# Decoder trunk on one core: B turned by transposes, norm weights applied from PSUM, x loaded over 128 partitions, two low parts and the first load of h moved

## The chip, the cores and the metric

The kernel runs on one core of a Trainium2 chip. The metric is the device time of one execution in microseconds (us). Five engines work side by side, each through its own instructions in order: TensorE (PE, matmuls and transposes, with weight loads as PEld), VectorE (DVE), ScalarE (ACT), GpSimd (POOL) and SyncE (SP, which here only issues DMAs). They meet through semaphores. PE writes to PSUM, of which this kernel uses eight banks of 128x512 float32; POOL works on SBUF alone.

## The reference, cut to what matters

A decoder of two layers over 256 tokens with 2048 features, all in float32: an S5 state-space mixer with GLU, a SwiGLU, sliding-window attention, a second SwiGLU, a norm ahead of each and one at the end. The change lies in the first layer's mixer and at the start of its GLU:

```python
hn = rmsnorm(h, norm_mix[0])                       # x * rsqrt(mean(x*x) + eps) * g
dt = exp(log_step); lb = exp(lam * dt)             # 128 groups x 64 states, complex
q  = (lb - 1) / lam                                # = (n_re, n_im) * conj(lam) / |lam|^2
bu = einsum('blgc,gpc->blgp', hn, q * b)           # 16 channels a group into 64 states
s  = associative_scan(lb, bu)                      # s[l] = lb * s[l-1] + bu[l]
y  = Re(einsum('blgp,gcp->blgc', s, c)) + d_skip * hn
gl = gelu(y) @ w_glu                               # 2048 x 4096
h  = x + gl[:, :2048] * sigmoid(gl[:, 2048:])
```

## The kernel before, in words

**The mixer** is `s5` (from L182). The tokens are cut into 64 chunks of L = 4. For each group the four tokens of a chunk are folded into one input of the state: X holds B times the powers of lb, so the state is scanned once a chunk, 63 steps, in two halves `hf` of the states. The order of work is written out by hand: inside `s5` the engines are wrapped in `Ordered`, whose instructions keep program order while `on` is true (so most rows of this stretch carry its line, L210); where it is off a scheduler places them.

The steps, with the names of the diff and the profile:
- `Bn` is B as loaded (128 groups on partitions), real, imaginary and real again. `turned_b` (L388) turns it into `B1` and `B2` (states on partitions), four channels to a PSUM bank `ps`. Before, each of its 32 products is a matmul of Bn with `wd[:, c]`, the identity scaled by one column of the norm weight `wg`; 16 ACT copies (L291) make `wd`. So the norm weight sits in B. ACT evicts each bank, with a sign (`sgn`) for B2.
- `LP` are the powers of lb, computed on DVE (L320 to L358) from `exp(ls)`. `q_` is q, from the inverse square `iv` (L366 to L378). PE turns LP into `LR`, `LI` and `pl`; ACT copies `LRs` and `LPT`.
- `real_parts(t)` on POOL: three products `tmp` of LRs with B1 for quarter t. `imag` on DVE: products `pa` of LI (in PSUM) with B2. `token(t, j)` adds the two into X; `last_token(t)` is a copy of B1 on ACT.
- `xk` is x by chunk and token, its two halves of features on partitions 0 to 63 and 64 to 127. `squares(j)` on ACT sum the squares of token j, `both` adds the two halves of a row on PE (`rb`), and a chain on DVE and ACT gives the scale `r0`. `scaled(hf, j)` writes r0 times xk to `xs`; `tokens(t, b)` turns xs on PE (`pu`) and ACT copies it to `U`.
- `turned_x` (PE `px`, ACT `xt`), `added` (PE `pv`) and `kept` (copy to V) follow for four quarters t and four blocks b. `kept(1, 3)` completes the first half's inputs V0, `kept(3, 3)` the second's, V1.
- `step(hf)` (L552 to L557) is one step of the scan: three DVE instructions on a bank `scan` and V. The first half leads by 20 steps. POOL meanwhile computes T (`first_states`, L704 to L709), four quarters.
- When the first half is done, ACT copies states to `St` (L772), PE multiplies U by `M` (`own_tokens`, L763) and St by T (`outputs`, L785) into `py`, ACT applies GELU, PE turns it (`turned`), and `gt` gets a high and a low part.

**Weights.** The class `Weights` streams 4096-wide weights as pieces of 512x512 (1 MB): `load` issues the DMA into one of two `raw` buffers, `high(i)` (ACT, L122) rounds it to a high part, `low(i)` (DVE unless told otherwise, L127) takes the rest. A raw buffer is free for the next load after its low part, and SP issues in order. A piece on PE is 24 matmuls of 128x512 (L911 to L913). Pieces 0 to 3 (`early_piece`) run between the parts of `s5`; pieces 4 to 7 open `glu` (L1015), which also loads x again into `h` (`load_h`), 512 columns at a time, as work `left` over between pieces.

## Time and profile before

| | |
|---|---|
| median of 3 runs (lowest to highest) | 2049.35 us (2048.52 to 2049.42) |
| profiled execution | 2049.24 us |
| its span, first to last instruction | 2047.5 us |
| PE, DVE, ACT, POOL busy | 1994.3 (97%), 1084.9 (53%), 868.7 (42%), 104.1 (5%) us |
| mean granted PE clock | 0.990 |

Busy time by stretches of the span, in us:

| stretch | PE | DVE | ACT | POOL | PE clock | DMA, GB/s |
|---|---|---|---|---|---|---|
| 0 to 50 | 34.56 | 34.08 | 33.00 | 26.31 | 0.93 | 114 |
| 50 to 110 | 46.00 | 53.85 | 34.24 | 45.72 | 0.83 | 33 |
| 110 to 150 | 32.70 | 20.10 | 23.35 | 24.95 | 0.96 | 81 |
| 150 to 200 | 46.58 | 25.62 | 21.86 | 5.48 | 0.97 | 200 |

A row of the timeline reads: start and duration in us, engine, line, operation, output<-inputs, shapes (partitions x elements), count of merged instructions, and in brackets how long the engine had been idle and what ended that.

### The profile page before, as it was taken

To read this page: it belongs to the slowest core of one execution; us is meant where nothing else is said; L and a number is where in the kernel's file an instruction comes from. 1 tells how busy PE (TensorE), PEld (TensorE's weight loads), DVE (VectorE), ACT (ScalarE), POOL (GpSimd) and SP (SyncE) were. 2 spreads that over 40 slices of the span, in tenths; PEclk is the share of its full clock that TensorE was granted. 3 is DMA by queue.
4 is the path that set the end of the run, shared out by engine and by line. 5 is a ranking of instruction groups with operands and counts; after the bars stand their busy time and mean duration, and the time that the engine had idled before them with its cause. 6 is when DMAs were issued, how large, how long until landed. Compare 5 with 4: busy or idle time off the path is not lost.

```text
span 2047.5 us, 25176 instructions
## 1 busy us (share of the span) xinstructions
PE 1994.3 (97%) x10668; PEld 1650.8 (81%) x10668; DVE 1084.9 (53%) x1341; ACT 868.7 (42%) x891; POOL 104.1 (5%) x70
## 2 busy tenths in 40 slices
PE   6789999999999999999999999999999999999998
PEld 6677888888888888888887777888888888888886
DVE  6855445544544454445466775544454455444545
ACT  6554444333333433433455454444333433333333
POOL 5761000000000000000000000000000000000000
PEclk9899999999999999999999999999999999999999
DMA  4026666555655565556564425555555665655564
GB/s 120 29 64 216 196 202 195 188 186 186 201 188 186 190 200 185 187 194 195 176 198 156 144 83 164 185 185 189 196 190 187 193 195 186 190 196 189 185 197 152
DMA packets 183600, 360.63 MB, mean 176 GB/s; under 512 B 10688, under 2 KB 10752, under 8 KB 183360
## 3 DMA queue, kind: packets, MB, share of 16 engines
q1 hardware_dynamic: 182336, 355.56, 53.8%
q8 instruction: 83, 1.36, 0.3%
q10 hardware_dynamic: 720, 2.14, 0.3%
q0 software_dynamic: 432, 1.33, 0.2%
q14 instruction: 29, 0.24, 0.0%
HBM read 356.91 MB, written 2.10 MB: 175 GB/s over the span
## 4 chain that ended last, share of the span: by engine, by line
PE 90%; POOL 3%; DVE 3%; DMA 2%; ACT 1%; issue 1%; SPq 0%; DVEq 0%; ACTq 0%; POOLq 0%
PE acc L913 28%; PE acc L911 28%; PE acc L912 28%; DMA raw<-in_s_w_glu_dram 1%; PE tr L1050 1%; POOL tmpT L704 1%; POOL T L705 1%; DVE w L127 1%; PE tr L955 1%; POOL T L707 1%; PE po L1197 0%; ACT w L122 0%; PE tr L1186 0%; DMA xk<-in_x_dram 0%; POOL T L709 0%
## 5 line engine op out<-in xcount | busy, mean ns | idle before, releaser
L127 DVE TENSOR_TENSOR w<-raw,w 128x2048 fp32r<-128x2048 f32 x329 | 754.0, 2292 | 830.7 <-ACT w L122 830.6
L122 ACT ACTIVATE w<-raw 128x2048 fp32r<-128x2048 f32 x332 | 636.3, 1916 | 980.6 <-PE acc L913 868.6
L911 PE MATMUL acc<-w,xT 128*128 128x512 f32 x1568 | 612.8, 391 | 0.0
L913 PE MATMUL acc<-w,xT 128*128 128x512 f32 x1568 | 611.3, 390 | 0.0
L912 PE MATMUL acc<-w,xT 128*128 128x512 f32 x1568 | 610.6, 389 | 0.0
L913 PEld LDWEIGHTS acc<-w,xT 128*128 128x128 f32 x1568 | 294.3, 188 | 62.0 <-issue 1.0
L911 PEld LDWEIGHTS acc<-w,xT 128*128 128x128 f32 x1568 | 294.4, 188 | 61.3 <-issue 1.3
L912 PEld LDWEIGHTS acc<-w,xT 128*128 128x128 f32 x1568 | 294.5, 188 | 60.7 <-issue 0.5
L911 PE MATMUL acc<-w,hT 128*128 128x512 f32 x704 | 275.2, 391 | 0.0
L912 PE MATMUL acc<-w,hT 128*128 128x512 f32 x704 | 273.6, 389 | 0.0
L913 PE MATMUL acc<-w,hT 128*128 128x512 f32 x704 | 273.4, 389 | 0.0
L911 PEld LDWEIGHTS acc<-w,hT 128*128 128x128 f32 x704 | 132.2, 188 | 28.1 <-ACT hT L1052 1.2
L913 PEld LDWEIGHTS acc<-w,hT 128*128 128x128 f32 x704 | 132.1, 188 | 27.7
L912 PEld LDWEIGHTS acc<-w,hT 128*128 128x128 f32 x704 | 132.2, 188 | 26.9
L912 PE MATMUL acc<-w,gt 128*128 128x512 f32 x256 | 100.5, 392 | 2.4 <-POOL w L127 1.8
L911 PE MATMUL acc<-w,gt 128*128 128x512 f32 x256 | 100.7, 394 | 0.0
L913 PE MATMUL acc<-w,gt 128*128 128x512 f32 x256 | 100.0, 391 | 0.0
L912 PEld LDWEIGHTS acc<-w,gt 128*128 128x128 f32 x256 | 48.4, 189 | 13.0 <-POOL w L127 2.3
L1077 DVE TENSOR_TENSOR h<-h,acc 128x512 f32<-128x512 f32 x64 | 43.4, 687 | 24.7 <-PE acc L913 24.7
L911 PEld LDWEIGHTS acc<-w,gt 128*128 128x128 f32 x256 | 48.3, 189 | 10.1
L913 PEld LDWEIGHTS acc<-w,gt 128*128 128x128 f32 x256 | 48.4, 189 | 10.0
L1063 ACT ACTIVATE act<-acc,ry 128x512 f32<-128x512 f32 x44 | 30.1, 690 | 59.9 <-PE acc L913 59.9
(243 smaller groups left out, 1260.6 us busy)
## 6 DMA issues: line engine op xcount, KB each, us to landing
raw<-in_ffn_w_gate_dram SPq DMA_DIRECT2D x88, 1024.0 KB, 5.2
raw<-in_ffn_w_up_dram SPq DMA_DIRECT2D x88, 1024.0 KB, 5.2
raw<-in_ffn_w_down_dram SPq DMA_DIRECT2D x88, 1024.0 KB, 5.1
raw<-in_s_w_glu_dram SPq DMA_DIRECT2D x32, 1024.0 KB, 5.3
raw<-in_attn_w_qkv_dram SPq DMA_DIRECT2D x20, 1024.0 KB, 5.1
raw<-in_attn_w_o_dram SPq DMA_DIRECT2D x16, 1024.0 KB, 5.1
xk<-in_x_dram SPq DMA_DIRECT2D x8, 256.0 KB, 8.1
h<-in_x_dram SPq DMA_DIRECT2D x8, 256.0 KB, 5.8
```

Of the source, the lines that this page charges most:

```text
L122: keep(S.activation(w[:, 0], self.raw[i], AF.Copy))
L127: keep(e.tensor_tensor(lo, self.raw[i], hi.bitcast(F32), op=ALU.subtract))
L704: PL.tensor_tensor(tmp, cr, l0, op=ALU.mult)
L705: PL.tensor_tensor(o[:, :, ri], ci, l1, op=ALU.mult)
L707: PL.tensor_tensor(o[:, :, ri], o[:, :, ri], tmp, op=ALU.add)
L911: keep(PE.matmul(acc, x_[:, 0], w[0][:, a], start=first, stop=False))
L912: PE.matmul(acc, x_[:, 0], w[1][:, a], start=False, stop=False)
L913: PE.matmul(acc, x_[:, 1], w[0][:, a], start=False, stop=last)
L955: PE.transpose(pt[:, t], h[t][:, kt * P : (kt + 1) * P], ident)
L1050: PE.transpose(pt[:, a], hm[t][:, a * P : (a + 1) * P], ident)
L1063: S.activation(s, pg[t], AF.Silu, scale=r[0][:, t : t + 1])
L1077: V.tensor_tensor(hc, hc, acc[t], op=ALU.add)
```

## The change

- `turned_b` transposes Bn with the plain identity (`ident`); `wd`, `wg` and the 16 copies go. The order of evictions and squares is written out anew, and the last two banks of B2 are evicted by DVE.
- The norm weight is loaded as `nrow` (two rows of 1024) and spread over the partitions by two matmuls with `sel` into two PSUM banks `gb`. `scaled` now multiplies xk by r0 and by gb in one instruction (scalar_tensor_tensor), all on DVE: 8 of 128x256 for the first half of the features and 4 of 128x512 for the second, where ACT and DVE had 8 of 128x512.
- x is loaded with four DMAs over 128 partitions in place of eight over 64: partition 2k + h now holds half h of chunk k, and `both`, `pu` and the strides follow.
- q_'s eight products go from DVE to POOL, ahead of `real_parts`; its inverse square is worked in between the first operations of `exp`.
- `kept(1, .)` goes from DVE to ACT, `LPT`, `scan_tables(0)` and `imag_and_tokens` change places; `drows` is a copy, since its input is weighted already, and one small DMA (`wrow`) goes.
- Behind `early_piece(gt, 0, 0, last)`: `W.low(2)` goes from POOL to DVE, `W.high(3)` and `W.low(3)` (POOL) move up to it, ahead of the state copies.
- `glu` pops one piece of left-over work after each of pieces 4 to 7, where it popped all of it after piece 7.

The first place where rows move is the start of ACT, from the copies `wd` on. Before:

```order
L210 ACTIVATE wd<-ident,wg 128x128 x16
L210 COPY Bn<-Bn 128x1024
L210 ACTIVATE B_5_260<-ps_261 128x128x4
L210 ACTIVATE B_5_260<-ps_267 128x128x4
L210 ACTIVATE B_5_260<-ps_273 128x128x4
L210 ACTIVATE B_5_260<-ps_279 128x128x4
L210 ACTIVATE U,ssq<-xk 128x1024
L210 ACTIVATE B_10_286<-ps_287,sgn 128x128x4
L210 ACTIVATE B_10_286<-ps_293,sgn 128x128x4
L210 ACTIVATE U,ssq<-xk 128x1024
L210 ACTIVATE B_10_286<-ps_300,sgn 128x128x4
L210 ACTIVATE B_10_286<-ps_306,sgn 128x128x4
```

And now, from the copy of Bn on:

```order
L210 COPY Bn<-Bn 128x1024
L210 COPY B_7_244<-ps_246 128x128x4
L210 ACTIVATE U,ssq<-xk 128x1024
L210 COPY B_7_244<-ps_253 128x128x4
L210 COPY B_7_244<-ps_259 128x128x4
L210 ACTIVATE U,ssq<-xk 128x1024
L210 COPY B_7_244<-ps_266 128x128x4
L210 ACTIVATE B_8_245<-ps_272,sgn 128x128x4
L210 ACTIVATE U,ssq<-xk 128x1024
L210 ACTIVATE B_8_245<-ps_279,sgn 128x128x4
L210 COPY LRs<-LR_297 128x384
L210 ACTIVATE U,ssq<-xk 128x1024
```

The copies of the identity are gone, the squares stand one eviction or more earlier, and LRs comes behind six evictions, where it came behind eight and three squares.

The second is ACT behind the low parts of gt's second piece, where the state copies St of the second half and the high parts stand. Before (w_1869 is piece 3, w_174 piece 4):

```order
L807 CAST gt_1828<-pt_1831 128x512
L772 COPY St_1850<-V_78 128x32x28
L772 COPY St_1851<-V_78 128x32x28
L772 COPY St_1850<-V_78 128x32x24
L772 COPY St_1851<-V_78 128x32x24
L122 ACTIVATE w_1869<-raw_1807 128x2048
L772 COPY St_1850<-V_78 128x32x8
L772 COPY St_1851<-V_78 128x32x8
L772 COPY St_1850<-V_78 128x32x4
L772 COPY St_1851<-V_78 128x32x4
L122 ACTIVATE w_174_1988<-raw_1809 128x2048
```

And now (w_1839 is piece 3, w_176 piece 4):

```order
L820 CAST gt_1816<-pt_1819 128x512
L122 ACTIVATE w_1839<-raw_1795 128x2048
L785 COPY St_1842<-V_78 128x32x28
L785 COPY St_1843<-V_78 128x32x28
L785 COPY St_1842<-V_78 128x32x24
L785 COPY St_1843<-V_78 128x32x24
L785 COPY St_1842<-V_78 128x32x8
L785 COPY St_1843<-V_78 128x32x8
L785 COPY St_1842<-V_78 128x32x4
L785 COPY St_1843<-V_78 128x32x4
L122 ACTIVATE w_176_1976<-raw_1797 128x2048
```

The high part of piece 3 stands ahead of all eight copies. On DVE the low part of piece 2 now stands between gt's low parts and the last twelve steps of the scan.

The third is SP at the start of `glu`. Before (raw_2235 is piece 8, raw_2322 piece 11):

```order
L109 DMA raw_2179<-in_s_w_glu_dram 128x4x512
L109 DMA raw_2235<-in_s_w_glu_dram 128x4x512
L109 DMA raw_2264<-in_s_w_glu_dram 128x4x512
L109 DMA raw_2293<-in_s_w_glu_dram 128x4x512
L109 DMA raw_2322<-in_s_w_glu_dram 128x4x512
L1020 DMA h_2229<-in_x_dram 128x512
L1020 DMA h_2230<-in_x_dram 128x512
L109 DMA raw_2367<-in_s_w_glu_dram 128x4x512
```

And now (raw_2223 is piece 8):

```order
L109 DMA raw_2167<-in_s_w_glu_dram 128x4x512
L109 DMA raw_2223<-in_s_w_glu_dram 128x4x512
L1031 DMA h_2217<-in_x_dram 128x512
L1031 DMA h_2218<-in_x_dram 128x512
L109 DMA raw_2254<-in_s_w_glu_dram 128x4x512
L109 DMA raw_2283<-in_s_w_glu_dram 128x4x512
L109 DMA raw_2312<-in_s_w_glu_dram 128x4x512
L109 DMA raw_2355<-in_s_w_glu_dram 128x4x512
```

The two loads of h's first 512 columns have passed three weight loads.

The diff, cut to its core:

```diff
-            wg = ep.tile([G, GC], F32, name="wg")
+            nrow = ep.tile([2, D // 2], F32, name="nrow")
...
-            nc.scalar.dma_start(wg, norm_mix[0].rearrange("(g c) -> g c", c=GC))
+            nc.scalar.dma_start(nrow, norm_mix[0].rearrange("(h d) -> h d", h=2))
...
             for j in range(L):
-                for ph in range(2):
-                    nc.sync.dma_start(xk[ph * NK : (ph + 1) * NK, j], xv[:, j, ph * (D // 2) : (ph + 1) * (D // 2)])
+                nc.sync.dma_start(xk[:, j], xv[:, j].rearrange("k (h d) -> k h d", h=2))
...
-            wd = ep.tile([G, GC, G], F32, name="wd")
-            for c in range(GC):
-                S.activation(wd[:, c], ident, AF.Copy, scale=wg[:, c : c + 1])
             S.copy(Bn[:, 2], Bn[:, 0])
+            gb = [bank([P, 512], "gb") for _ in range(2)]
+            for hf in range(2):
+                PE.matmul(gb[hf], sel.rearrange("p k h -> p (k h)"), nrow[:, 512 * hf : 512 * hf + 512],
+                          start=True, stop=True)
...
+            PL.tensor_tensor(u, LP[:, 0, 1], aim, op=ALU.mult)
...
+            PL.tensor_tensor(q_[:, 1], u, iv, op=ALU.mult)
...
-                    for c in range(4):
-                        PE.matmul(pt[:, c], b[:, :, 4 * i + c], wd[:, 4 * i + c], start=True, stop=True)
-                    S.activation(o[:, :, 4 * i : 4 * i + 4], pt.rearrange("p c g -> p g c"), AF.Copy, scale=scale)
...
+                for c in range(4):
+                    PE.transpose(pt[:, c], b[:, :, 4 * i + c], ident)
+                evict(o[:, :, 4 * i : 4 * i + 4], pt.rearrange("p c g -> p g c"))
...
+            for i in (2, 3):
+                turned_b(B2, i, lambda o, v: V.tensor_scalar(o, v, sgn[:, 1:2], None, ALU.mult))
...
+            def scaled(hf, j, t=None):
+
+                a = slice(0, 32) if t is None else slice(16 * t, 16 * t + 16)
+                v, w = (o.rearrange("p (a c) -> p a c", c=GC)[:, a]
+                        for o in (xk[:, j, 512 * hf : 512 * hf + 512], gb[hf]))
+                V.scalar_tensor_tensor(xs[:, hf, :, :, j].rearrange("p a g c -> p (a g) c")[:, a],
+                                       v, r0[:, j : j + 1], w, ALU.mult, ALU.mult)
...
-            kept(1, 0, V.tensor_copy)
+            kept(1, 0, S.copy)
...
             early_piece(gt, 0, 0, last)
+            W.low(2, pin)
+            W.high(3, pin)
+            W.low(3, pin, PL)
             for q in (1, 3):
                 St[q] = big([P, 2, 16, NK], "St")
             copies_so_far()
-            W.low(2, pin, PL)
-            more(4)
-            copies_so_far()
-            W.high(3, pin)
-            W.low(3, pin, PL)
...
                     piece(accs[half], gt[q], q == 0, q == 3)
-                while left:
-                    left.pop(0)()
+                    if left:
+                        left.pop(0)()
```

More of the change, by code (lines that the diff above doesn't have):

```diff
@@ L272, in s5 @@
                 V.memset(sgn[NS:, i : i + 1], 2 * i - 1.0)
-            both = sp.tile([P, 2, NK], F32, name="both")
+            both = sp.tile([P, NK, 2], F32, name="both")
             for i in range(2):
-                V.tensor_tensor(both[:, i], ident[:, :NK], ident[:, NK:], op=ALU.add)
+                V.tensor_tensor(both[:, :, i], ident[:, 0::2], ident[:, 1::2], op=ALU.add)
+            sel = sp.tile([2, NK, 2], F32, name="sel")
+            V.tensor_copy(sel, bc(ident[:2, :2], 1, NK))
             for hf in range(2):
@@ L302, in small, with exp @@
                 return ep.tile(shape, dt, name=f"sm{n_small[0]}")
-            def exp(t, shape):
+            def exp(t, shape, between=None):
                 a, n, r, p = small(shape), small(shape), small(shape), small(shape)
-                V.tensor_scalar(a, t, -87.0, 88.0, ALU.max, ALU.min)
+                first = V.tensor_scalar(a, t, -87.0, 88.0, ALU.max, ALU.min)
+                if between:
+                    pin(first)
+                    between()
                 V.tensor_scalar(n, a, 1.4426950408889634, MAGIC, ALU.mult, ALU.add)
@@ L319, in s5, with one_over_square @@
             sh = [G, NS]
-            dt_ = exp(ls, [G, 1])
-            V.on = False
+            den, iv, v = (sp.tile(sh, F32, name=f"den{i}") for i in range(3))
+            def one_over_square():
+                pin(V.tensor_tensor(den, are, are, op=ALU.mult))
+                pin(V.tensor_tensor(v, aim, aim, op=ALU.mult))
+                V.tensor_tensor(den, den, v, op=ALU.add)
+                V.reciprocal(iv, den)
+            dt_ = exp(ls, [G, 1], one_over_square)
             ard = small(sh)
@@ L385, in squares, with turned_b, negated @@
                 S.activation(U[:, j].rearrange("p a k -> p (a k)"), xk[:, j], AF.Square, accum_out=ssq[:, j : j + 1])
[L388 to L401 removed]
+            B1, B2 = big([P, G, GC], "B1"), big([P, G, GC], "B2")
+            def turned_b(o, i, evict):
+                f = 0 if o is B1 else 1
+                b = Bn[:, f : f + 2].rearrange("p r s c -> p (r s) c")
+                pt = bank([P, 4, G])
+                for c in range(4):
+                    PE.transpose(pt[:, c], b[:, :, 4 * i + c], ident)
+                evict(o[:, :, 4 * i : 4 * i + 4], pt.rearrange("p c g -> p g c"))
+            def negated(o, v):
+                S.activation(o, v, AF.Copy, scale=sgn[:, 1:2])
+            turned_b(B1, 0, S.copy)
+            squares(0)
+            turned_b(B1, 1, S.copy)
+            turned_b(B1, 2, S.copy)
+            squares(1)
+            turned_b(B1, 3, S.copy)
+            turned_b(B2, 0, negated)
+            squares(2)
+            turned_b(B2, 1, negated)
+            for i in (2, 3):
+                turned_b(B2, i, lambda o, v: V.tensor_scalar(o, v, sgn[:, 1:2], None, ALU.mult))
             LR, LI = bank([P, 3, G], "LR"), bank([P, 3, G], "LI")
@@ L448, in token @@
                                 tmps[t][:, j].rearrange("p h f c -> p (h f) c"), op=ALU.add)
-            for t in range(2):
-                real_parts(t)
-                last_token(t)
+            real_parts(0)
             squares(3)
+            last_token(0)
+            LPT = sp.tile([P, L, 2, PAIRS], F32, name="LPT")
+            S.copy(LPT, pl)
+            real_parts(1)
             imag(0, 2)
@@ L561, in lead @@
                     step(0)
-            PL.tensor_tensor(drows[:, :, 3], drow.rearrange("a (g c) -> a g c", g=2),
-                             wrow.rearrange("a (g c) -> a g c", g=2), op=ALU.mult)
             for t in (2, 3):
                 real_parts(t)
+            PL.tensor_copy(drows[:, :, 3], drow.rearrange("a (g c) -> a g c", g=2))
             def imag_and_tokens(t):
@@ L590, in s5 @@
             tokens(1, 1)
+            for j in range(L):
+                scaled(1, j)
             turned_x(1, 0)
@@ L596, in s5 @@
             added(1, 0)
+            kept(1, 0, S.copy)
             turned_x(1, 2)
             added(1, 1)
-            for j in (2, 1):
-                imag(3, j)
-            token(3, 2)
-            kept(1, 0, V.tensor_copy)
+            kept(1, 1, S.copy)
+            scan_tables(0)
             turned_x(1, 3)
-            scaled(1, 0, S)
             added(1, 2)
-            token(3, 1)
-            kept(1, 1, V.tensor_copy)
-            imag(3, 0)
+            kept(1, 2, S.copy)
             added(1, 3)
-            kept(1, 2, V.tensor_copy)
-            token(3, 0)
-            kept(1, 3, V.tensor_copy)
+            kept(1, 3, S.copy)
             idm = sp.tile([P, GC], F32, name="idm")
@@ L615, in s5 @@
             V.on = False
-            for j in (1, 2, 3):
-                scaled(1, j, S)
+            imag_and_tokens(3)
             Cq = big([G, GC, 2, NS], "Cq")
```

59 lines of the change are left out of this document (17 added, 42 removed).

## The prediction

> **What bounds the kernel now.** I read the page, then the busy time by stretches (columns: stretch, length, busy PE, PEld, DVE, ACT, POOL, clock, DMA share, GB/s), then what PE waited for between 90 and 200 us (total, times, longest), then the timeline backwards from each wait.
>
> ```profile
> 200.00:2047.00 1847.00, 1834.48 (x8425) 1512.98 (x8423) 951.27 (x824) 756.20 (x710) 1.63 (x3) 1.00 0.57 184
> ...
> PE pm L741 <- ACT k L734: 11.3, 1, 11.3
> PE py L763 <- issue: 4.0, 1, 4.0
> PE tr L955 <- DVE h L1038: 2.9, 1, 2.9
> PE acc L912 <- POOL w L127: 1.8, 1, 1.8
> ```
>
> From 200 us on PE is busy for all but 12.5 of 1847 us, and the change puts nothing there. So the forecast is how much earlier that stage begins. The 11.3 us are no cost of their own: PE has run ahead and waits, through ACT, for the scan on DVE.
>
> ```profile
> 65.86 0.58 ACT L210 COPY V<-pv 128x504 f32<-128x504 f32 x1 [0.59 <-PE pv L210]
> 66.47 0.30 DVE L552 TENSOR_TENSOR scan<-scan,V 128x128 f32<-128x128 f32 x1 [3.99 <-ACT V L210]
> 90.00:100.00 10.00, 0.00 (x0) 0.00 (x0) 10.00 (x67) 2.21 (x3) 9.84 (x6) 0.63 0.00 0
> ```
>
> The last copy into V, `kept(3, 3)` at 65.86, is the hinge. The scan of both halves starts behind it and keeps DVE full (10.00 of 10 us at 90), and w0's high part, with which POOL's long run on w and T starts, follows it on ACT. What moves the hinge moves both.
>
> **The front: the hinge moves by 8.4 us.**
>
> ```profile
> 2.12 0.43 SPq L248 DMA_DIRECT2D Bn<-in_s_b_im_dram  x1
> Bn<-in_s_b_im_dram SPq DMA_DIRECT2D x1, 512.0 KB, 5.8
> 8.06 14.19 PE L210 MATMUL ps<-wd,Bn 128*128 128x128 f32 x64 [8.06 <-ACT wd L210]
> 15.29 0.60 ACT L210 ACTIVATE B<-ps 128x512 f32<-128x512 f32 x1 [1.04 <-PE ps L210]
> 22.29 0.69 ACT L210 ACTIVATE B<-ps,sgn 128x512 f32<-128x512 f32 x1 [1.06 <-PE ps L210]
> 23.91 0.47 ACT L210 COPY LRs<-LR 128x384 f32<-128x384 f32 x1
> 25.31 1.06 ACT L210 ACTIVATE U<-xk 128x1024 f32<-128x1024 f32 x1
> 26.27 0.19 ACT L210 ACTIVATION_READ_ACCUMULATOR U<-xk 128x1 f32 x1
> 28.61 2.45 DVE L210 TENSOR_SCALAR xs<-xk,r 128x512 f32<-128x512 f32 x2
> 30.98 0.68 DVE L210 TENSOR_TENSOR X<-pa,tmp 128x512 f32<-128x512 f32 x1
> 31.21 1.94 PE L210 MATMUL pu<-ident,xs 128*128 128x128 f32 x8 [4.31 <-DVE xs L210]
> 33.12 1.76 PE L210 MATMUL px<-ident,X 128*128 128x128 f32 x8
> ```
>
> Now PE turns B in 14.19 us and ACT waits 1.04 to 1.06 us ahead of most evictions. A transpose costs 0.24 (1.94 over 8, half clock), so a group of four 0.97, and PE gets ahead. B lands at 2.12 + 5.8 = 7.9; the wd copies are gone and gb's two matmuls run before. The first eviction starts at 8.9 and from there ACT sets the pace: four copies of 0.60, two signed ones of 0.69, three squares of 1.06 + 0.19, together 7.5, so LRs runs at 16.4 to 16.9 (now it ends at 24.38) and the fourth square ends at 18.1 (now 26.46). The last two evictions go to DVE, which now waits there for LI, so they cost nothing; were DVE late, LI's first product would be later by twice 0.68.
>
> Two things could hold this up.
>
> ```profile
> DMA to landing us min/median/max: 6.4/8.1/9.1
> ...
> 13.87 0.28 DVE L358 TENSOR_TENSOR LP<-LP,cm 128x128 f32<-128x128 f32 x1
> 30.74 0.42 POOL L210 TENSOR_TENSOR drows<-drow,wrow 64x32 f32<-64x32 f32 x1
> ```
>
> x: now the first of eight pieces lands at 9.0 (2.6 + 6.4) and the last, issued at 7.9, by 17.0, some 1.1 a piece. A square needs two of them. At that rate the first square would start at 10.1 rather than 9.5 and the fourth at 17.0 rather than 16.9, so the load costs ACT 0.6 at the worst; four transfers over all partitions can only take that away, and a load faster than ACT's own work is worth nothing more. I leave it out of the sum and in the range. POOL now computes q_ between LP (14.15) and real_parts: eight small products at 0.42 at most, 3.4, so until 17.5, 0.6 behind LRs; the first token needs one product of 128x512 more (1.2, half of the 2.42 that POOL's L709 takes below for twice the size): 18.7, where the sum for the scale wants DVE at 18.5. At most 0.2, left out.
>
> From the end of the fourth square to xs the row of now takes 2.15 (26.46 to 28.61); with the token's 0.6 on DVE r0 is there at 20.9. Then four new products of 128x256, one operand in PSUM. No row has these; the nearest is
>
> ```profile
> 190.53 1.65 DVE L959 SCALAR_TENSOR_TENSOR xT<-tr,gcol,xT 128x256 fp32r<-128x256 f32 x4
> ```
>
> 0.41 each, and upwards half of what 128x512 costs now, 0.61. I take 0.41 (same operation, size and a PSUM operand): 22.5. X, pa and X add 0.6, 0.6, 0.68: px starts at 24.4, against 33.12, 8.7 earlier.
>
> Behind px PE itself is the pace: it is full until
>
> ```profile
> 49.03 1.09 PE L210 MATMUL pu<-ident,xs 128*128 128x128 f32 x8 [1.18 <-ACT xs L210]
> ...
> 34.00:38.00 4.00, 3.97 (x77) 0.93 0.00 0
> ```
>
> The wait of 1.18 goes, since ACT no longer writes xs there; ACT now has the copies `kept(1, .)`, X and U in a row instead, which I put at 0.8. The mean clock of 0.93 over 34 to 38 is half speed until 34.6 and full from there, 3.4 after PE began with pu; px ran 1.5 us cold. In the changed kernel PE begins near 22.5 and rises between 26 and 29: some 2 us more at half clock, a third of which PE loses, 0.7. 8.7 + 1.2 - 0.8 - 0.7 = 8.4. With 0.61 for each new product DVE gets late for the px of t = 1 and the scan: 6.2. With a clock that rises at once and no wait on ACT: 10.
>
> A rule speaks against turning B by transposes. The Trainium skill (TensorE: Matmul & The Clock Gate, Part 4) says that a transpose does not count as busy for the clock. By that row it does: from 31.21 to 34.6 PE ran pu and px alone, transposes all, and the clock rose. By the rule the clock would rise only a window of 3.4 after pv has begun, PE would lose a third of that, 1.1, and the hinge would gain 7.3 in place of 8.4.
>
> **w2's low part and the state copies: 0.5 us.**
>
> ```profile
> 117.11 2.28 DVE L127 TENSOR_TENSOR w<-raw,w 128x2048 fp32r<-128x2048 f32 x1
> 117.25 4.38 POOL L707 TENSOR_TENSOR T<-T,tmpT 128x1024 f32<-128x1024 f32 x1
> raw<-in_s_w_glu_dram SPq DMA_DIRECT2D x32, 1024.0 KB, 5.3
> ...
> 123.79 6.53 ACT L772 COPY St<-V 128x896 f32<-128x896 f32 x4 [2.52 <-POOL tmpT L704]
> 123.84 2.42 POOL L709 TENSOR_TENSOR T<-T,tmpT 128x1024 f32<-128x1024 f32 x1
> 126.21 4.59 POOL L127 TENSOR_TENSOR w<-raw,w 128x2048 fp32r<-128x2048 f32 x1
> 132.78 0.22 DVE L557 TENSOR_TENSOR V<-V,scan 128x64 f32<-128x64 f32 x1
> 137.27 2.05 PE L785 MATMUL py<-T,St 64*64 64x64 f32 x128
> ```
>
> (Times here on the clock of before.) PE's piece 2 stood 1.8 us for POOL's 4.59. On DVE the low part comes behind gt's low parts and is there by 126, before PE wants it at 128.6. But twelve steps of the scan are queued behind it, and outputs(1) needs the last state: scan's end 133.0 + 2.28 = 135.3. DVE and POOL also stretch each other (4.38 where L709 takes 2.42); if DVE is the one that waits, up to 0.8 more: 136.1. W.high(3), now ahead of the state copies on ACT, waits for raw 3 (issued when DVE has w1's low part, 119.4, + 5.3 = 124.7) and ends the long copies at 133.5 rather than 130.3 (123.79 + 6.53), still before the scan. Two last copies, and outputs(1) starts at 136.8 rather than 137.27: 0.5 of the 1.8 is left; between 1.3 and -0.6. T of quarter 3, stretched to 128.4, is needed at 140 only.
>
> **The stall in PE's issue: 2.5 us.**
>
> ```profile
> 111.60 2.08 PE L785 MATMUL py<-T,St 64*64 64x64 f32 x125 [0.73 <-issue]
> 143.90 0.81 PE L763 MATMUL py<-M,U 64*64 64x64 f32 x20 [3.96 <-issue]
> q8 instruction: 1, 0.02, 1.0%
> GB/s 0 0 0 0 0 0 177 164 123 109 55 164 246 314 314 300 369 369 437 423 410 423 423 341 396 396 410 328 219 178 14 0 0 0 0 0 0 0 0 0
> ```
>
> The last two rows are of 137 to 143, the GB/s in 40 slices: raw 5 moves from 138 to 141.5, and with the one packet of the instruction queue PE goes on 2 us later. With no load near, such a wait took 0.73. Raw 5 follows W.low(3), which now runs straight behind T: 128.4 + 4.6 = 133, so it moves from 134 to 137.5, ahead of the fetch. Between 0 and 3.2; I take 2.5.
>
> **The first h: 2.3 us.**
>
> ```profile
> 176.01 1.92 ACT L122 ACTIVATE w<-raw 128x2048 fp32r<-128x2048 f32 x1 [0.72 <-DMA raw<-in_s_w_glu_dram]
> 180.70 0.97 SPq L1020 DMA_DIRECT2D h<-in_x_dram  x2
> ```
>
> h is issued behind raw 11 and lands too late. Now it stands behind raw 8, some 14 us earlier; raw 9 to 11 queue behind its 0.5 MB, 1.4 us at the 370 GB/s above. Raw 9 has its high part at 176.0 and PE wants w9 near 184: hidden, but ACT's sigmoid and DVE's sum follow it, so part of the wait may stay: 2.0 to 2.9 (the wait above), 2.3 taken.
>
> 8.4 + 0.5 + 2.5 + 2.3 = 13.7. The profiled execution took 2049.24 (span 2047.5; the median of the runs is 2049.35, no more than noise away): 2035.5.
>
> **Rivals.** (1) The fetch meets a raw load again, since every load of the stage moves too: the 2.5 is lost, 2038. For it: the 3.96 of now; against it: by the sum above raw 5 has moved before the fetch is due. (2) The front gives half, because gb holds two of the eight banks or the new products cost 0.61 and DVE is late for X: 4 to 6 in place of 8.4, 2038 to 2040. For it: PE, ACT and DVE hand eight banks round in that stretch, and each new wait lies on the path of px and pv; against: gb goes free after DVE's twelfth product, and POOL's products are ready long before. (3) Transposes don't raise the clock: 2036.6; the row at 34 to 38 is against it. (4) The load and order edits do what they say, but the hinge does not move, because scan and POOL wait for something that I hold to be early: 2044. (5) Slower: each of the six raw loads of the stage meets a fetch at 3.96 where one did; 5 x 3.96 = 19.8 against the 11.2 of the other terms gives 2058; it decides from the third further hit. Against it: one in six hit.
>
> **How the numbers follow.** Forecast 0.60 (its own range 2031 to 2038), (1) 0.15, (2) 0.12, (3) 0.04, (4) 0.05, (5) 0.04. All terms at their best ends sum to 17.4, 2031.8; (1) and (2) together reach 2042: range 2030.5 to 2042. 0.2% is 4.1 us, about what runs of this kernel can tell: faster below 2045.25, which is all but (5) and parts of (2) and (4): 0.92 faster, 0.04 no change, 0.04 slower.
>
> **What would show it.** LRs near 16.5, r0 near 21, px near 24.4, the last V copy near 57.5, the scan's two halves from there; no wait of PE on POOL's w; the issue wait near 1; tr with under 1 us of wait. A px later than 28, a V copy later than 61, or new issue waits of PE over 3 us would refute it.

## The result, and the profile after

The changed kernel takes 2031.65 us (median of 4 runs, 2030.9 to 2034.0), the kernel before 2049.05 beside it: a ratio of 0.9917 (95% interval 0.99 to 0.9934). The forecast was 2035.5 with a range of 2030.5 to 2042. The profiled execution took 2030.9, its span 2029.1, 18.4 less than before.

First the front, from the timeline of the changed kernel (start, duration, engine, line, operation, tiles, and in brackets the idle time before and what ended it):

```profile
7.46 6.03 PE L210 MATMUL ps<-ident,Bn 128*128 128x128 f32 x32 [0.58 <-DMA Bn<-in_s_b_im_dram]
8.58 0.59 ACT L210 COPY B<-ps 128x512 f32<-128x512 f32 x1 [1.47 <-PE ps L210]
9.07 1.06 ACT L210 ACTIVATE U<-xk 128x1024 f32<-128x1024 f32 x1
14.77 0.50 ACT L210 COPY LRs<-LR 128x384 f32<-128x384 f32 x1
19.12 1.66 DVE L210 SCALAR_TENSOR_TENSOR xs<-xk,r,gb 128x256 f32<-128x256 f32 x4
22.93 1.94 PE L210 MATMUL px<-ident,X 128*128 128x128 f32 x8
38.69 1.09 PE L210 MATMUL pu<-ident,xs 128*128 128x128 f32 x8
55.94 0.58 ACT L210 COPY V<-pv 128x504 f32<-128x504 f32 x1 [0.59 <-PE pv L210]
```

PE turns B in 6.0 us where it took 14.2, LRs runs at 14.77 where it ran at 23.91, px starts at 22.93 (33.12), pu at 38.69 no longer waits for xs, and the hinge, the last copy into V, stands at 55.94 (65.86).

Then the stage behind the scan, of the same timeline:

```profile
105.18 2.28 DVE L127 TENSOR_TENSOR w<-raw,w 128x2048 fp32r<-128x2048 f32 x1
105.21 4.18 POOL L717 TENSOR_TENSOR tmpT<-Cg,LPT 128x1024 f32<-128x1024 f32 x1
124.05 0.72 ACT L785 COPY St<-V 128x128 f32<-128x128 f32 x2 [0.40 <-DVE V L578]
124.61 2.10 PE L798 MATMUL py<-T,St 64*64 64x64 f32 x128 [0.17 <-ACT St L785]
129.78 1.15 PE L798 MATMUL py<-T,St 64*64 64x64 f32 x61 [2.08 <-issue]
133.48 0.34 PE L798 MATMUL py<-T,St 64*64 64x64 f32 x6 [0.45 <-issue]
136.60 1.03 PE L813 MATMUL pt<-ident,y 128*128 128x128 f32 x8
169.27 0.33 PE L966 MATMUL tr<-ident,h 128*128 128x128 f32 x1 [0.83 <-DVE h L1049]
```

PE no longer waits for POOL's w, outputs(1) starts 12.7 us earlier than before, the wait in PE's issue is 2.08 where it was 3.96, and the one for h is 0.83, with 0.27 a row later, where it was 2.87.

One thing more is gone, which the prediction did not price. The next rows are busy time in windows of 3.41 us, the raster on which the trace changes PE's clock (columns: stretch, length, busy PE, PEld, DVE, ACT, POOL, clock, DMA share, GB/s). Of the kernel before:

```profile
140.34:143.75 3.41, 0.00 (x0) 0.00 (x0) 0.00 (x0) 0.30 (x2) 0.00 (x0) 1.00 0.31 117
143.75:147.17 3.42, 3.27 (x91) 3.15 (x91) 0.00 (x0) 0.00 (x0) 0.00 (x0) 0.50 0.02 5
184.71:188.12 3.41, 0.54 (x4) 0.26 (x3) 3.20 (x3) 2.36 (x3) 0.00 (x0) 1.00 0.43 162
188.12:191.53 3.41, 3.41 (x13) 2.87 (x12) 3.41 (x5) 2.63 (x8) 0.00 (x0) 0.50 0.88 267
```

And of the changed kernel, around its longest wait:

```profile
128.26:131.67 3.41, 1.89 (x68) 1.82 (x69) 0.00 (x0) 0.11 (x1) 0.00 (x0) 1.00 0.02 5
131.67:135.08 3.41, 2.96 (x73) 2.37 (x72) 1.29 (x2) 2.13 (x6) 0.00 (x0) 1.00 0.00 0
```

Before, each of the two long waits was followed by a window at half clock in which PE was busy (3.27 and 3.41 us, half of which is lost: 3.3 in all). In the changed kernel the waits are shorter and no window of the stage is slow.

### The profile page after: what moved, and what is told of

The parts are those of the page before. It is cut to its first block, busy times and chain, and to the rows that moved or that the text cites. A ratio compares the mean times of both kernels' runs of the same rounds, so it can differ in the third digit from the quotient of the medians.

```text
span 2029.1 us, 25100 instructions
## 1 busy us (share of the span) xinstructions
PE 1984.3 (98%) x10640; PEld 1638.7 (81%) x10640; DVE 1088.9 (54%) x1343; ACT 860.1 (42%) x871; POOL 103.7 (5%) x77
## 4 chain that ended last, share of the span: by engine, by line
PE 91%; DVE 6%; ACT 1%; DMA 1%; issue 1%; POOL 0%; DVEq 0%; ACTq 0%
PE acc L922 29%; PE acc L924 29%; PE acc L923 28%; DVE scan L573 1%; DVE w L127 1%; PE tr L1061 1%; DVE V L578 1%; DVE V L576 1%; DMA raw<-in_s_w_glu_dram 1%; PE pv L210 1%; PE tr L966 1%; PE po L1208 1%; PE tr L1197 0%; PE py L798 0%; ACT sc L1181 0%
## 5 line engine op out<-in xcount | busy, mean ns | idle before, releaser
L923 PEld LDWEIGHTS acc<-w,gt 128*128 128x128 f32 x256 | 48.1, 188 | 10.6 <-DVE w L127 1.0
```

The lines of the kernel that those rows point to most:

```text
L923: PE.matmul(acc, x_[:, 0], w[1][:, a], start=False, stop=False)
```

## The experiments

All are compared with the changed kernel's 2031.65. The kernel before was run beside each group of them, and its median moved: 2049.05 beside the changed kernel, 2048.48 beside e1 to e4, 2049.82 beside e6, e7, e9 and e10, 2049.14 beside e5, e11 and e12, 2047.79 beside e13. So a difference of 1 to 2 us between groups says little, and where it matters the gain on the kernel before beside it is given; the changed kernel's gain is 17.4. Because single executions differ by up to 5 us, each kernel's trace says more than its time. This table cuts every profiled execution at the same four points: the last copy into V; from there to outputs(1); from there to the second pt of end(1, 3); from there to the end of the span. The last column counts windows at half clock between 110 and 200 us. Seven of the kernels share the changed front (changed, e1, e2, e5, e7, e9, e10); their last copy into V lies between 55.39 and 56.40, so a difference of 1 us in that column is within what executions of one front differ by.

| kernel | last copy into V | to outputs(1) | to second pt | to the end | half-clock windows |
|---|---|---|---|---|---|
| before | 65.86 | 71.41 | 14.48 | 1895.75 | 2 |
| changed | 55.94 | 68.67 | 11.99 | 1892.50 | 0 |
| e1_h_late | 56.40 | 70.58 | 10.42 | 1896.20 | 1 |
| e2_low_back | 56.28 | 73.17 | 12.46 | 1892.69 | 2 |
| e3_b_matmul | 62.74 | 73.02 | 10.97 | 1892.57 | 0 |
| e4_x_64 | 57.09 | 70.60 | 11.47 | 1894.84 | 1 |
| e5_front_only | 55.39 | 71.37 | 14.00 | 1893.14 | 1 |
| e6_warm | 57.22 | 70.57 | 10.96 | 1892.75 | 0 |
| e7_shift | 55.84 | 70.88 | 15.19 | 1892.99 | 2 |
| e9_hold | 56.16 | 68.92 | 11.72 | 1892.30 | 0 |
| e10_raw5 | 56.29 | 68.75 | 11.72 | 1892.04 | 0 |
| e11_before_fill | 66.36 | 71.33 | 14.59 | 1897.42 | 2 |
| e12_all | 55.23 | 71.94 | 10.82 | 1892.21 | 0 |
| e13_line | 55.19 | 69.37 | 10.65 | 1895.39 | 1 |

### The first h late again (e1_h_late)

```diff
                     piece(accs[half], gt[q], q == 0, q == 3)
-                    if left:
-                        left.pop(0)()
+                while left:
+                    left.pop(0)()
```

> The changed kernel with one part undone: the first load of h is issued after piece 7 again, as before the change. Theory A (the late h costs its wait and, through that wait, clock): PE's wait for h ahead of tr goes from 1.1 us back to about 2.9, and the clock falls to half for one of its windows behind it, as it did before at 188 to 192 us, which costs PE about 1.4 to 1.7 more: 3.2 to 3.5 us above the changed kernel, about 2035. Theory B (only the wait, as the prediction priced it): 1.8 to 2.3 us above, and no fall of the clock. Everything ahead of 150 us stays where it was.

2033.39 (2032.44 to 2035.36), 1.7 above the changed kernel, and its gain 2.3 less: the median is what theory B expects, not the 3.2 to 3.5 of theory A. In the profiled execution, its slowest, both halves of theory A are there: the timeline has

```profile
105.67 2.03 POOL L717 TENSOR_TENSOR tmpT<-Cg,LPT 128x1024 f32<-128x1024 f32 x1
105.93 3.93 DVE L127 TENSOR_TENSOR w<-raw,w 128x2048 fp32r<-128x2048 f32 x1
126.98 2.10 PE L798 MATMUL py<-T,St 64*64 64x64 f32 x128 [2.08 <-ACT St L785]
130.81 1.15 PE L798 MATMUL py<-T,St 64*64 64x64 f32 x61 [0.74 <-issue]
173.92 1.11 PE L966 MATMUL tr<-ident,h 128*128 128x128 f32 x4 [3.32 <-DVE h L1049]
```

and a window at half clock at 173.7; from the second pt to the end it takes 3.7 longer than the changed kernel, of which the longer wait is 2.2 and the rest, 1.5, falls to the clock. By the median not all executions pay it, which no second trace shows. The first three rows were not expected, since nothing was changed there: w1's low part on DVE took 3.93 where the changed kernel shows 2.28, and PE waited 2.08 for the last state copy. POOL had begun its product 0.26 us earlier; in the changed kernel's trace DVE began 0.03 earlier, and POOL took 4.18 for what takes 2.03 here. The fourth row is a compensation: since outputs(1) came 2.4 later, raw 5's load was over, and the issue wait was 0.74.

### The low parts of w2 and w3 as before (e2_low_back)

```diff
-            W.low(2, pin)
-            W.high(3, pin)
-            W.low(3, pin, PL)
             for q in (1, 3):
                 St[q] = big([P, 2, 16, NK], "St")
             copies_so_far()
+            W.low(2, pin, PL)
+            more(4)
+            copies_so_far()
+            W.high(3, pin)
+            W.low(3, pin, PL)
```

> The changed kernel with one part undone: w2's low part on POOL again and behind the state copies, w3's high and low part behind it. Theory A (this reordering is worth 2.7 us ahead of outputs(1), and raw 5's load, which it moves, sets the length of PE's issue wait): outputs(1) starts 2.2 to 2.7 us later against the last copy into V, PE waits 1.8 us for POOL's w, and the issue wait behind outputs(1) goes from 2.1 back to about 4: 4 to 5 us above the changed kernel, about 2036. Theory B (the prediction's 0.5 for the reordering and 2.5 for the stall): 3.0 above. Theory C (the gain behind the hinge came with the earlier front and not from this order): at most 1 above, issue wait still near 2.

2035.59 (2034.86 to 2037.8), 3.9 above. PE waits for POOL's w again, even longer than before the change:

```profile
121.42 0.50 PE L925 MATMUL acc<-w,gt 128*128 128x512 f32 x1 [2.94 <-POOL w L127]
134.35 1.15 PE L798 MATMUL py<-T,St 64*64 64x64 f32 x60 [1.82 <-issue]
```

Its issue wait is 1.82 rather than the 4 that theory A expected, but a window at half clock follows it, and another follows the wait for w at 122.12. The windows of this kernel around it:

```profile
132.36:135.77 3.41, 1.59 (x73) 1.39 (x66) 0.00 (x0) 0.46 (x2) 0.00 (x0) 1.00 0.02 5
135.77:139.18 3.41, 3.41 (x72) 2.96 (x71) 1.39 (x2) 1.21 (x3) 0.00 (x0) 0.50 0.02 5
```

From the last copy into V to the second pt it takes 85.6, the kernel before 85.9, the changed kernel 80.7. So this reordering carries the whole 5 us of that stretch: theory A's total, and C falls. Its parts are not A's: outputs(1) stands 4.5 later against the last copy into V, where 2.2 to 2.7 was expected.

One more kernel, e5_front_only, also has h's first load late again, so that the changed front alone is left. Expected was 2038.5 to 2040 if the terms add up (theory A), with waits of 2 to 3 us for POOL's w, 2 to 4 for the fetch and 3 for h, and 2040.5 to 2041.5 if the front gives only the 8.4 of the prediction (theory B). It took 2038.53 (2035.75 to 2038.59), a gain of 10.6: at the edge of theory A. In its profile, the fastest execution, PE waits 1.04 for w, 3.34 in issue and 1.77 for h, all in place and two of them shorter than expected. By these gains the front carries 10.6 of the changed kernel's 17.4, and the edits behind it the other 6.8.

### B turned by matmuls (e3_b_matmul)

```diff
-                    PE.transpose(pt[:, c], b[:, :, 4 * i + c], ident)
+                    PE.matmul(pt[:, c], b[:, :, 4 * i + c], ident, start=True, stop=True)
```

> The changed kernel with B turned by 32 matmuls with the identity in place of 32 transposes; all else as changed. Theory A (PE's turning of B was the pace of the front): a matmul costs 0.44 us where a transpose costs 0.19, so PE's 32 take 14.2 us rather than 6.0, LRs comes 7 to 8 us later (near 22.5 rather than 14.8), and the last copy into V with it: 7 to 8 us above the changed kernel, about 2039. Theory B (ACT's squares and the load of x were the pace): 1 to 3 us above.

2040.52 (2038.21 to 2043.16), 8.9 above: theory A. The front of this kernel:

```profile
7.29 14.20 PE L210 MATMUL ps<-ident,Bn 128*128 128x128 f32 x64 [0.39 <-DMA Bn<-in_s_b_im_dram]
22.34 0.48 ACT L210 COPY LRs<-LR 128x384 f32<-128x384 f32 x1 [3.62 <-PE LR L210]
```

By the table the hinge is 6.8 later than in the changed kernel: so much of its 9.9 us are the transposes. A further 4.35 lie between the hinge and outputs(1), which the expectation did not have: the 32 rows more on PE move its issue waits (1.25 us ahead of the first pt), w1's low part takes 4.19, and PE waits 2.23 for St.

### x over 64 partitions (e4_x_64)

```diff
-                nc.sync.dma_start(xk[:, j], xv[:, j].rearrange("k (h d) -> k h d", h=2))
+                for ph in range(2):
+                    nc.sync.dma_start(xk[64 * ph : 64 * ph + 64, j],
+                                      xv[32 * ph : 32 * ph + 32, j].rearrange("k (h d) -> k h d", h=2))
```

> The changed kernel with x loaded by eight DMAs over 64 partitions each in place of four over 128 (the same bytes to the same places). Theory A (the load now sets the squares, since ACT got ahead of the prediction): pieces land some 1.1 us apart, the fourth square starts near 17 rather than 15.1, r0 and the last copy into V come 1 to 2 us later: 2033 to 2034. Theory B (the prediction: the load costs ACT 0.6 at the worst): 0 to 0.6 us above the changed kernel.

2031.58 (2031.15 to 2035.8): the time says theory B, no difference. The trace has the delay of theory A: the sum for the scale waits for ACT's squares, `17.60` where the changed kernel has 16.38, and the hinge comes 1.15 later.

```profile
17.60 0.38 PE L210 MATMUL rb<-ssq,both 128*128 128x4 f32 x2 [2.21 <-ACT U L210]
```

So the load delays the scale by 1.2 us and the hinge by some 0.7 to 1.7 against the seven kernels with the changed front, more than the 0 to 0.6 of the prediction; in the time this lies within what executions of one kernel differ by.

### Fillers that keep the clock up at the front, eight of them (e6_warm)

```diff
             PE.matmul(pss, both.rearrange("p a k -> p (a k)"), ssq, start=True, stop=True)
+            for _ in range(8):
+                PE.matmul(LR[:, 3], ident, ident, start=True, stop=True)
```

(LR has a fourth column block for it, which is not read.)

> The changed kernel with eight matmuls of the identity with itself put on PE behind the sum for the scale (into columns of a bank that nothing reads), where PE otherwise idles 4.2 us for xs and its clock falls to half from about 19.5 to 26 us. They fill 3.5 us at full clock and end before xs is there. Theory A (the half clock sets the start of the px and pv stretch, the prediction's 0.7 and more): px's eight transposes take 1.1 us rather than 1.94, the first 32 products of pv 1.15 rather than 1.62, and the last copy into V comes 1.2 to 1.5 us earlier, and the whole with it: about 2030.3. Theory B (ACT's evictions and DVE's products are the pace there): the clock is full, and the last copy into V moves by less than 0.4.

2032.7 (2031.67 to 2034.86), and the hinge 1.3 later, against both theories.

```profile
16.71 2.03 PE L210 MATMUL LR<-ident 128*128 128x128 f32 x16
20.97 1.06 PE L210 MATMUL pu<-ident,xs 128*128 128x128 f32 x8 [2.23 <-DVE xs L210]
```

The fillers took 2.03 us rather than 3.5: 0.127 a row, where I had taken the 0.22 of the matmuls with Bn (14.20 over 64). PE still idled 2.23, and the half clock only moved from 19 to 26 us to 22 to 29, onto px and pv. The question stayed open until e12_all.

### POOL held behind DVE (e9_hold)

```diff
             first_states(1)
-            first_states(3)
...
             last = end(0, 2)
+            first_states(3, gt[0][:, 1, 3, T - 1 :].bitcast(F32))
...
+                    if behind is not None and ri == 0:
+                        PL.tensor_copy(tmp[:, 0, 0, :1], behind)
                     PL.tensor_tensor(tmp, cr, l0, op=ALU.mult)
```

> The changed kernel; POOL's last quarter of T (first_states(3)) starts with a copy of one column of gt's low part into its buffer, so that POOL cannot begin there before DVE goes on to w1's low part. In three of five profiles so far POOL began first and DVE's low part took 3.9 to 4.1 us where it takes 2.28, the last state copy came 2 us later and PE waited 2.1 us for it; in the changed kernel's own profile DVE began first by 0.03 us and POOL took 4.18 where it takes 2.04. Theory A (the engine that begins first runs through, the other waits): the low part takes 2.28 in the profile, PE waits under 0.5 for St ahead of outputs(1), and the runs lie closer together at the lower end of the changed kernel's, 2030 to 2031.5. Theory B (the two stretch each other for a reason that order does not set): low parts of 3 to 4 us stay, and the time is that of the changed kernel, 2031 to 2034.

2033.01 (2030.88 to 2034.44): the time is theory B's. In the trace theory A holds:

```profile
105.42 2.28 DVE L127 TENSOR_TENSOR w<-raw,w 128x2048 fp32r<-128x2048 f32 x1
105.63 2.11 POOL L718 COPY tmpT<-gt 128x1 f32<-128x1 f32 x1 [0.29 <-DVE gt L823]
```

A copy of a single column takes POOL 2.11 us, until DVE's low part is over at 107.70: the engine that begins second does not run slower, it waits. The Trainium skill (SBUF — State Buffer, SBUF: two separate sides) calls the port pair of the two an exclusive lock, held by whichever starts first for its whole instruction; this trace agrees, with 2.28 for the first and 2.11 for a copy behind it. But the second half of theory A failed: the executions did not come closer together, so this order is not what spreads them.

### Raw 5's load held as well (e10_raw5)

```diff
             last = end(1, 3, lambda: own_tokens(3))
+            def behind_gt():
+                t = pp.tile([P, 4, 512], F32, tag="raw", name=nm("raw"), bufs=2)
+                pin(S.copy(t[:, 0, :1], gt[1][:, 0, 1, T - 1 :].bitcast(F32)))
+                return t
+            W.early[5] = behind_gt
+            W.cap = 10 ** 9
+            W.load(6)
```

(with `cap`, 5 until here, as a further bound in `load`)

> As the run before (POOL held), and raw 5's load is held back as well: ACT copies one column of gt's second tile into the raw buffer first, so the load begins near 132 us, not near 123. Theory A (PE's issue wait is its instruction fetch, which lands behind raw 5's 1 MB when the two meet): the wait of 2.1 us behind outputs(1) falls to 0.7 to 0.8, as where no load is near, and the time by 1.3 against the run before; raw 5 lands near 137.5, its high part at 139.5, its low part before PE wants piece 5 near 146. Theory B (the wait belongs to that place in the code): it stays at 2, and the later load costs 0 to 1.

2030.58 (2030.27 to 2031.0), a gain of 19.2, and with e12_all the least spread. Its issue wait, though, is 1.52, not 0.7:

```profile
129.65 0.56 PE L801 MATMUL py<-T,St 64*64 64x64 f32 x22 [1.52 <-issue]
```

The DMA view of the stretch 124 to 129 (GB/s in 40 slices) shows why half of theory A stands. Of this kernel, where the only packet is the instruction fetch:

```profile
GB/s 0 0 0 0 0 0 0 0 0 0 0 0 0 0 0 0 0 0 0 0 0 0 131 0 0 0 0 0 0 0 0 0 0 0 0 0 0 0 0 0
```

And of the changed kernel, where the fetch begins at 127.4, inside the end of raw 5's load (to 127.7):

```profile
GB/s 33 164 164 164 66 164 82 180 147 164 344 360 377 426 410 426 410 393 410 393 426 360 475 410 410 393 361 312 82 16 0 0 0 0 0 0 0 0 0 0
```

The boundary ahead of the one where PE waits lies 67 rows of 16.4 ns (2.10 over 128) into outputs(1), and the fetch follows it: without the load from 126.1 to 126.9, 0.7 us; with it from 125.7 to 127.4, 1.7. So the load does delay the fetch. But PE went on 2.8 us after the packet began here, and 2.4 after it there; why is open, and the wait is only 0.3 shorter than in e9_hold. The lower median against e9_hold (2.4) can't be put down to it from these traces.

### PE's rows shifted by 64 (e7_shift)

```diff
+                        for _ in range(extra if t2 == e == 0 else 0):
+                            PE.matmul(pm[:, 0, 0, :1], ident, ident[:, :1], start=True, stop=True)
                         for jj in range(2):
                             PE.matmul(pm[:, jj], shifts[2 * e + jj], ...)
...
-                    M[1] = kernels(lags, pin)
+                    M[1] = kernels(lags, pin, 32)
```

(on top of e9_hold)

> As the run with POOL held; and 32 products of one column (64 rows of PE in the trace) go into PE's wait for k near 82 to 95 us, where they cost nothing. They move every boundary of PE's instruction lines 64 rows ahead; in the trace the issue waits lie 127 to 128 rows apart. Theory A (the fetch is asked for one line ahead, and lands behind raw 5's load if it is asked for while that moves): the issue wait of 2.1 us in outputs(3) goes away from that place and one of about 3 us comes 64 rows earlier, in the second half of outputs(1): 0.8 to 1.5 us above the run with POOL held. Theory B (waits belong to the place in the code): it stays at row 3 of outputs(3) with 2.1.

2035.66 (2034.15 to 2036.9), 2.65 above e9_hold. Theory A:

```profile
126.72 2.09 PE L802 MATMUL py<-T,St 64*64 64x64 f32 x128 [1.43 <-ACT St L789]
132.27 1.03 PE L780 MATMUL py<-M,U 64*64 64x64 f32 x29 [3.38 <-issue]
```

The executions of the two kernels overlap a little (2034.15 to 2036.9 against 2030.88 to 2034.44). The wait stands 3 rows behind outputs(1) where it stood 67 behind (64 rows of own_tokens(3) and 3 of outputs(3)): the 64 added rows earlier. It is 3.38, and two windows at half clock follow. It costs more than the 0.8 to 1.5 expected for that reason.

### The wait for h filled, in the kernel before (e11_before_fill)

```diff
+            if not (n or a or g):
+                for _ in range(10):
+                    tc.keep_in_program_order(PE.matmul(pt[:, 2], ident, ident, start=True, stop=True))
             for t in range(2):
                 PE.transpose(pt[:, t], h[t][:, kt * P : (kt + 1) * P], ident)
```

> The kernel before the change with one addition: ten matmuls of the identity with itself (20 rows of 0.127 us, 2.5 us at full clock, into columns of a bank that nothing reads) stand on PE ahead of the first transposes of h, where PE idles 2.87 us for h. h is as late as before. Theory A (a wait of PE costs a second time: a window of 3.4 us in which PE stood idle for some 1.8 us or more is followed by one at half clock): PE's clock stays full from 188 to 192 us, its products there take 0.39 again in place of 0.63 to 0.77, and the time falls by 1.5 to 1.7 against the kernel before, though nothing arrives earlier. Theory B (the late h costs its wait alone, and the half clock there has another cause): no change, or up to 0.3 more for fillers that run over.

2050.56 (2048.33 to 2051.51); against its neighbours of the kernel before a ratio of 1.0004 (0.9995 to 1.0013). It decides nothing: in the profiled execution h came later than before, PE still idled 1.94 behind the fillers, and the half clock followed at 189.9.

```profile
183.96 2.39 PE L956 MATMUL tr<-ident 128*128 128x128 f32 x20
188.29 0.33 PE L959 MATMUL tr<-ident,h 128*128 128x128 f32 x1 [1.94 <-DVE h L1042]
```

### Sixteen fillers at the front, POOL and raw 5 held (e12_all)

The diffs of e9_hold, e10_raw5 and e6_warm together, with `range(16)`.

> The changed kernel with POOL held and raw 5 held as above, and sixteen matmuls of the identity with itself on PE behind the sum for the scale, where eight left 2.2 us of idle time and the half clock came 3 us later: 32 rows of 0.127 us fill all of the 4.1 us until xs is there. Theory A (the idle time sets the clock): no half clock between 16 and 30 us, pu and px take 1.06 to 1.09 for eight, the first pv 1.15, and the last copy into V comes 1.2 to 2 us before the 56.3 of the run with POOL and raw 5 held: 2028.6 to 2029.4. Theory B (ACT and DVE are the pace behind px): the clock is full, the last copy into V within 0.4 of 56.3, 2030.3 to 2030.8.

2031.72 (2031.28 to 2032.02), 1.1 above e10_raw5 and outside both ranges, though the hinge is 1.06 earlier:

```profile
16.39 3.82 PE L211 MATMUL LR<-ident 128*128 128x128 f32 x32
20.96 1.07 PE L211 MATMUL pu<-ident,xs 128*128 128x128 f32 x8 [0.75 <-DVE xs L211]
104.72 0.33 PE L803 MATMUL py<-T,St 64*64 64x64 f32 x3 [1.53 <-issue]
```

PE's clock stays full from 10.9 to 79.2 us, so filling the idle time kept it up (theory A there), and full clock at px is worth some 1.06 at the hinge, the spread of equal fronts being 1.0. The gain went in the last row: 32 more rows on PE move the fetch boundaries, and a wait of 1.53 came to stand ahead of the first pt (104.98, 102.83 in e10_raw5). Two low parts and the scan are queued on DVE behind what follows it.

### A whole instruction line of fillers (e13_line)

```diff
-                    M[1] = kernels(lags, pin)
+                    M[1] = kernels(lags, pin, 48)
```

(as in e7_shift, with 64x64 products, on top of e12_all)

> The run with POOL and raw 5 held and sixteen fillers, and 48 more products of one column (64x64, 96 rows of PE) in PE's wait for k. That run had its last copy into V 1.06 us earlier, yet was 1.1 slower than without the fillers: its 32 extra rows moved PE's issue waits, and one of 1.53 us came to stand ahead of the first pt, with gt's low parts, two low parts of weights and the scan behind it on DVE. Now 128 rows are added in all. Theory A (an instruction line is 128 rows of PE, and only the place of its boundaries cost the gain): the issue waits stand again where the run without fillers has them (94 rows into outputs(0), none of over 1 us ahead of pt), the first pt comes near 101.8, and the time is 2029.2 to 2029.8. Theory B (the earlier hinge is worth nothing, because DVE's scan or POOL's T sets what follows): 2030.3 to 2031, with the issue waits back in place or not.

2030.37 (2029.35 to 2032.42), at the lower end of theory B's range, while the trace has the waits and nearly the first pt of theory A (102.37 for 101.8). The boundaries are back where they were without fillers, to the row:

```profile
100.71 1.73 PE L805 MATMUL py<-T,St 64*64 64x64 f32 x98 [0.79 <-issue]
102.37 1.09 PE L820 MATMUL pt<-ident,y 128*128 128x128 f32 x8
128.66 1.15 PE L805 MATMUL py<-T,St 64*64 64x64 f32 x61 [1.01 <-issue]
162.92 1.92 ACT L123 ACTIVATE w<-raw 128x2048 fp32r<-128x2048 f32 x1 [6.22 <-DMA raw<-in_s_w_glu_dram]
169.01 0.33 PE L982 MATMUL tr<-ident,h 128*128 128x128 f32 x1 [1.92 <-DVE h L1065]
```

x98 and x61 are the groups of the changed kernel, so a line is 128 rows of PE. The second pt stands at 135.21, 1.55 ahead of e10_raw5. The last two rows show where that went: ACT's sigmoid for h stands behind a high part which waits for its load and starts at 162.92, as it does in the changed kernel (163.17), however early PE is. PE waited 1.92 for h, and a window at half clock followed. The median is the lowest of all kernels run, but so is that of the kernel before beside it: the gain is 17.4, the changed kernel's and e12_all's, and less than e10_raw5's 19.2. So the trace shows where theory A's gain went, and no gain is left in the time.

## Why the prediction was right, and where it was not

The time lies inside the range, and the forecast's sign and main term are right. Its sum was 13.7; the medians differ by 17.4, the profiled executions by 18.4. That is the prediction's 17.4 with every term at its best end (2031.8), and 1.15 above the lower end of its range: that the range held is in part luck, since two terms came out beyond their own best ends (1.3 for w2's low part, 2.9 for h), and the half clock behind the two waits was no term at all.

| step of the prediction | forecast | measured |
|---|---|---|
| the hinge moves | 8.4 | 9.9 |
| w2's low part and the state copies | 0.5 | 2.7 |
| the stall in PE's issue, with the clock behind it | 2.5 | 2.5 |
| the first h, with the clock behind it | 2.3 | 3.25 |

**The hinge moves by 8.4.** The mechanism is right and e3_b_matmul shows it (6.8 of it is the transposes). The mis-sized term is ACT's pace, "together 7.5": from the first eviction at 8.58 to LRs at 14.77 it is 6.2. I summed durations, and ACT begins the next row some 0.1 before the last one ends (8.58 + 0.59 against 9.07), twelve times. With B landed 0.5 earlier px came 1.5 ahead of the forecast. From px to the hinge, forecast and measurement are 33.1 and 33.0, so the 1.2, 0.8 and 0.7 there came out right together, though none was measured alone: the 0.7 is how much more the half clock costs than before, and the 1.06 of e12_all is all that it costs now. The x load's "0.6 at the worst" is 1.15 by e4_x_64. The new products took the 0.41 taken (1.66 over 4), and PE shows no wait on a bank: rival (2) fell, as did (4).

**w2's low part and the state copies: 0.5.** The step that failed is "scan's end 133.0 + 2.28", which would be 125.4 on the changed kernel's clock; V's last step ended at 124.0, and outputs(1) waited 0.17. The forecast moved the scan by the hinge alone, 9.9. But gt's low parts, which stand ahead of it on DVE, came 11.8 to 11.9 earlier: the turns on PE that feed them start 10.9 to 11.0 earlier, and two issue waits of 0.73 and 0.76 us ahead of the first low part had become one of 0.34. That the low part of w2 took 2.86 rather than 2.28 gave 0.6 of it back. In four of the profiles above (e1, e4, e6, e7) POOL or a fetch got in first, PE waited 1.4 to 2.2 for St, and there the term is 0.5 to 0.8, near the forecast; in e12_all and e3_b_matmul, with a fetch wait ahead of the first pt, it is -0.5 and -1.6. So the term goes by what gets in first, and the prediction had one such order.

**The stall in PE's issue: 2.5.** The number is right and its parts are not. "Raw 5 moves from 134 to 137.5, ahead of the fetch" failed: in the changed kernel the fetch still lies in the end of that load, and rival (1) is half true. The wait fell by 1.9 only, a new one of 0.45 came, and the 1.0 that is left over falls to the half-clock window that no longer follows. So the number is right by luck.

**The first h: 2.3.** The wait fell by 1.8 (2.87 to 0.83 and 0.27). The rest, 1.5, is put down to the second half-clock window: from the second pt to the end, the profiles without one take 1892.0 to 1893.1, those with one 1894.8 to 1897.4, except where it lay ahead of the second pt.

Rival (3), that transposes don't raise the clock, has nothing for it here. Two stretches of the changed kernel in which PE turns B:

```profile
8.00:12.00 4.00, 4.00 (x21) 4.00 (x20) 3.90 (x28) 3.42 (x6) 0.35 (x1) 1.00 1.04 403
12.00:16.00 4.00, 3.88 (x68) 3.62 (x66) 3.75 (x13) 4.00 (x9) 2.28 (x8) 1.00 1.21 228
```

All 21 rows of the first are transposes. Its 1.00 is no reading, though: the trace's first record of the clock is at 12.21 (at 14.05 in the kernel before, so that the 0.93 of its first 50 us is too high as well), and the view counts what lies ahead as full. The starts of the transposes lie 0.213 us apart until 12.18 and 0.113 from there, so the clock was half, and it rose at 12.21, behind a window of 3.41 us in which PE did nothing but transposes. Of rival (5) nothing was seen.

## What to carry to other kernels

Where PE is full behind it, price a wait of PE twice: as its own length, and, where it takes over half of one clock window (1.82 of 3.41 us here), as half of the next window as well. From the second pt to the end, the kernels before, e1, e4 and e13 took 1.5 to 1.8 us more than the changed kernel, over and above their longer waits for h. Sum a pipelined engine's rows by the distance of their starts, not by their durations. Adding or removing instructions on PE moves every later instruction fetch, so before an order that gained nothing is given up, the waits in its issue want a look: they may stand in a worse place than before.

## What the runs showed of the hardware

- **The clock.** Cut on the trace's own raster of 3.41 us, all fourteen profiles have 24 windows between 96 and 196 us at full clock in which PE idled 1.2 us or more. The 11 with 1.82 to 3.41 us of idle time were each followed by a window at half clock; the 13 with 1.24 to 1.81 by one at full clock. This holds for that stretch alone. Between 60 and 85 us, eleven windows with 0 to 1.01 us idle were followed by half clock; PE worked there mainly on products of 16 columns (pk) or of one. At the front, one with 1.83 (e11_before_fill) and one with 1.96 (e4_x_64) were followed by full clock. So idle time as the views count it is not all that sets the clock, and what else does stays open. The Trainium skill (TensorE: Matmul & The Clock Gate, What's actually happening) gives the window as 3413 ns and free-running, which agrees, and lets the clock fall after a window that is idle; in that stretch 1.82 us of it were enough. Since the raster does not follow the program, a wait of about 2 us falls on either side (2.08 in the changed kernel without a drop, 1.82 in e2_low_back with one), which fits executions of one kernel that lie 0.7 to 5 us apart; a trace of two executions of one kernel that differ so was not taken, so this is argued and not shown.
- **The instruction fetch.** Issue waits lie 127 to 128 rows of PE apart, 64 added rows moved them by 64 (e7_shift), and 128 added rows left them in place. Behind outputs(1), in all fourteen profiles, the fetch starts 0.5 to 0.7 us after PE reaches the boundary ahead of it where raw 5's load is over or within 0.3 us of its end (e1, e3, e4, e6, e10, e12, e13), and 1.3 to 3.6 after it where its 1 MB still moves (before, changed, e2, e5, e7, e9, e11); PE goes on 2.2 to 2.8 after it starts.
- **DVE and POOL.** Whichever begins first runs through, and the other stands: 2.28 and 4.18 for DVE and POOL in one order, 3.93 and 2.03 in the other, for the same two instructions.
- **Turning B.** The transposes lie 0.213 us apart at half clock and 0.113 at full clock (changed kernel, either side of 12.21). The matmuls with Bn, two rows for each block where the transpose has one, lie 0.22 apart on both sides of 14.05 in the kernel before, where the record of full clock begins and the duration of a row falls from 0.42 to 0.38: their pace did not change there.
